# RWKV rounds of a hybrid trunk step emitted phase by phase, and two norm products moved to GpSimd

## The chip, the cores and the metric

The kernel runs on one core of one Trainium2 chip. The metric is the device time of one execution in microseconds (us); the kernel before was run three times. The engines are named as in the profile: PE is TensorE's matmul, PEld its weight load, DVE is VectorE, ACT is ScalarE, POOL is GpSimd, and SP (SyncE) issues most of the transfers.

## The reference

One step of a trunk of two layers. The even layer runs differential attention and a bidirectional RWKV-7 time mixing side by side; the change touches the RWKV part alone. For 1280 positions (1024 latent tokens in four blocks of 256, and 256 context tokens), 8 heads of 64 and two directions it computes:

```python
def wkv_scan(state0, r, w, k, v, kk, a):
    def step(S, inp):
        r_t, w_t, k_t, v_t, kk_t, a_t = inp
        sa = jnp.einsum("bhij,bhj->bhi", S, -kk_t)
        S = (S * w_t[:, :, None, :] + sa[..., None] * (kk_t * a_t)[:, :, None, :]
             + v_t[..., None] * k_t[:, :, None, :])
        return S, jnp.einsum("bhij,bhj->bhi", S, r_t)
...
    for d in range(2):
        w_raw = (P["rwkv_w0"][e, d] + jnp.tanh(wd[:, :, d]) @ P["rwkv_w2"][e, d]).astype(jnp.float32)
        decay = jnp.exp(-jnp.exp(-jax.nn.softplus(-w_raw) - 0.5))
        a = jax.nn.sigmoid(P["rwkv_a0"][e, d] + ad[:, :, d] @ P["rwkv_a2"][e, d])
        kd = k * (1 + (a - 1) * kvec[1])
...
        S, y = wkv_scan(s0[:, d], *inputs)
...
        ys = ys + y
        bonus = bonus + jnp.sum(rh * kdh * r_k, axis=-1, keepdims=True) * vh
    mu = jnp.mean(ys, axis=-1, keepdims=True)
    var = jnp.mean((ys - mu) ** 2, axis=-1, keepdims=True)
    yn = ((ys - mu) * lax.rsqrt(var + LNX_EPS)).reshape(b, L, B_WIDTH)
    y = (yn * lnx[0] + lnx[1] + bonus.reshape(b, L, B_WIDTH)).astype(fb.dtype) * g
```

## The kernel before

The scan is done in chunks of 32 positions. The RWKV stage has **five rounds**, q = 0 to 4. A round takes 256 positions of each direction (round 4 the context), which are 8 chunks of 8 heads in two directions. A round is split in two **halves** of four heads (half number n = 2q and 2q + 1), a half in two **pairs** of units (pair pp_ = 0, 1; a unit is two heads of one direction d).

The parts of a round, each written as a Python generator that yields between its pieces:

- **Preparation** of a half, `half_prep`: two pairs, each with two `unit_values` and two `unit_products`, so four steps a pair. A unit loads r, k and kkh (`piece_prep`; in rounds 0, 1 and 4, which are called fresh here, kkh is worked out: head sums L746/L808, a root with GpSimd's power L137, rsx L817, a flip on TensorE L753, kkh L820). Then come the small products lora_ps (L760, tanh on ScalarE L764), the scan sc (L842) and bk (L868, L874) on VectorE, kr, bkw and others on GpSimd (L839 to L878), the matrices G_ps (L897, masked into G on VectorE L901), the copies il (L904) and bd (L884) on ScalarE, bonus sums bon_ps (L746, L909) and flips of bkw (L753, copied into G on ScalarE L914).
- **Inverse** of the round, `inverses`: one VectorE chain of 31 steps over all units of the round. Each step has a product tm (L947) and an addition into x (L951), both with (31-kk)(kk+1) elements in 128 partitions. It begins with two transposes nn (L937, L938) and ends with xt and xn (L957, L958). It needs il of both halves.
- **Corrections** of a half, `corrections`: for each of four units GpSimd copies tz out of xt or xn (L984), and TensorE does mq_ps (L988), gv_ps (L993), ms_ps (L1000) and tb_ps (L1006), with ScalarE copies between. They load sv (L978).
- **Chains** of a half, `chains`: four steps, each with L1052 on TensorE, L1057 on VectorE, L1061 on TensorE, the new state (L1076) on VectorE, and the outputs y_ps (L1085, L1090) on TensorE. Chain 0 is the first half's, chain 1 the second half's. In round 4 a chain ends with four transposes of the states (sf_ps, L1113) and their stores (L1118).
- **Posts**, `post(q, d)`: the group norm of a finished block of 256 positions, done during the inverse of the next round (posts of round 2 in round 3, of round 3 in round 4; the last one behind round 4). It reads the array y (128 x 1024) and the values vb. Mean and variance are VectorE's (L1157), GpSimd does vb times the bonus (L1150), plus the bias (L1152) and the power ln_r (L137), and VectorE does y times ln_r (L1159), times the weight (L1160), plus vb (L1161) and, behind flips on TensorE, the gate product ob (L1168).
- **ada**: the blocks of adaLN weights. Each block has two 512 KB loads (ada_w, SP's queue, two buffers), matmuls L191, a copy L196 and small matmuls L200. It fills in wherever a `run` names it, so many steps a round.

`run` takes pairs of a generator and a count and interleaves their steps in proportion. What it emits is the program's order of priority. A scheduler then reorders the instructions of each engine by a simulated timeline, so the order on an engine is not the order of the code. All PSUM tiles of preparation, posts, corrections, ada and the states come from `ps_g`, one ring of three buffers that are handed out in the order of emission: a tile cannot be written before the one emitted three places earlier was read.

In a round, `pa_` is the preparation of the next round's first half, `pb_` that of its second half, `co[0]` and `co[1]` are the corrections of the halves, and `ch[0]` and `ch[1]` the chains. Before, pair 1 of `pa_` (four of its nine steps) is emitted beside the inverse, one step beside `co[0]`, and the other four beside chain 0 and `co[1]`. Half of `pb_` goes beside chain 1, the rest behind it.

Of the kernel before, what the change touches and what calls it, by code (L numbers as in the profile page):

```python
# [15 lines left out]
ALU = mybir.AluOpType  # L16
# [83 lines left out]
def hybrid_step(ctx: ExitStack, tc: tile.TileContext, i: dict, o: dict):  # L100
    nc = tc.nc
# [232 lines left out]
    with ExitStack() as st:  # L334
# [45 lines left out]
        with ExitStack() as st2:  # L380
            wp = pool(st2, "wv", side="right")
            for cb in range(4):
                raw = ww.tile([128, KD, 128], F32, tag="w_raw", bufs=3, name="v_raw")
                with tc.issue_after(first_ada):
                    nc.sync.dma_start(
                        out=raw,
# [7 lines left out]
                if cb % 2 == 1:  # L394
                    for ti in range(T // 128):
# [11 lines left out]
                        if ti >= LS // 128:  # L407
                            r0 = ti * 128 - LS
                            nc.gpsimd.dma_start(
                                out=o["cache_v"][0, 0, r0:r0 + 128].rearrange("t h d -> t (h d)")[:, cs], in_=vs  # L410
# [3 lines left out]
        with ExitStack() as st2:  # L414
# [35 lines left out]
            def do_fb(ti):  # L450
# [38 lines left out]
                out=nlam[:, 1:2], in0=ls[:, 0:1], scalar1=ls[:, 1:2], scalar2=LAM_INIT, op0=ALU.subtract, op1=ALU.add  # L489
# [177 lines left out]
    with ExitStack() as st:  # L667
# [26 lines left out]
        for a, x in enumerate((0.5, -0.5)):  # L694
# [6 lines left out]
            out=kv1h[:, 1, :], in0=kv[:, 1, :], scalar1=-0.25, scalar2=0.5, op0=ALU.mult, op1=ALU.add  # L701
# [2 lines left out]
        for p in range(4):  # L704
            nc.vector.tensor_scalar(out=bonk[:, p, :], in0=bones, scalar1=kv[:, 2, p:p + 1], scalar2=2.0, op0=ALU.mult, op1=ALU.mult)
        NP, NTP, NCP = 256, 2, 4
        A1, A2, A3, A4, A5 = 18, 4, 6, 6, 16
        cmask = eg.tile([128, NP], F32, name="cmask")
        nc.gpsimd.memset(cmask, 1.0)
        nc.gpsimd.memset(cmask.rearrange("p (c s) -> p c s", s=C)[:, :, 0:1], 0.0)  # L710
# [414 lines left out]
        def post(q, d):  # L1125
# [8 lines left out]
            vb = lt.tile([128, NTP, 512], F32, tag="vb", bufs=1, name="vb")  # L1134
# [4 lines left out]
            yf = y.rearrange("p a b s -> p a (b s)")  # L1139
# [11 lines left out]
            lv = lambda a: cst["lnx"][:, a, :].unsqueeze(1).to_broadcast([128, NTP, 512])  # L1151
# [5 lines left out]
                nc.vector.reduce_sum(var[:, a:a + 8], sq, axis=AX.X)  # L1157
            rsqrt(rs, var, 1.0 / 64, LNX_EPS, lt, NH2)
            nc.vector.tensor_tensor(out=yv, in0=yv, in1=bc(rs), op=ALU.mult)  # L1159
            nc.vector.tensor_tensor(out=yf, in0=yf, in1=lv(0), op=ALU.mult)  # L1160
            nc.vector.tensor_tensor(out=yf, in0=yf, in1=vb, op=ALU.add)  # L1161
            yield
            for p in range(4):
                gp = ps_g([128, NP], "gg_ps")
# [8 lines left out]
        def run(*gens):  # L1173

            todo = [[g, n, 0] for g, n in gens if n]
            while todo:
                t = min(todo, key=lambda t: (t[2] + 1) / t[1])
                t[2] += 1
                if next(t[0], 0) == 0 or t[2] == t[1]:
                    todo.remove(t)  # L1180

        none = iter(())
        ada = ada_blocks(
            [(0, j) for j in range(8, 24)] + [(1, j) for j in range(24)], ep, PG[0], "ada", 1, 2, 1
        )
# [16 lines left out]
        for q in range(5):  # L1202
            inv = inverses(R[q])
            pa_ = begin(2 * q + 2)
            ps_ = chain(*[post(*a) for a in posts.get(q - 1, ())])
            run((inv, 9), (pa_, 4), (ada, A1), (ps_, 16))
            if q == 4:
                for _ in ada:
                    pass
            co = [corrections(R[q], H[2 * q + e]) for e in range(2)]  # L1210
            ch = [chains(H[2 * q + e]) for e in range(2)]
            run((inv, 9), (co[0], 4), (pa_, 1), (ada, A2))
            y_tiles(q)
            run((ch[0], 5), (co[1], 4), (pa_, 4), (ada, A3))
            if q == 4:
                st_d.close()
                PG[:] = [pool(st, "pz", space=PSUM), 2]
                fw = pool(st_w, "fw1", side="right")
                out_weights(fw, pool(st_o, "ow", side="right"), range(KD))
                fo = pool(st_o, "of", side="right")  # L1220
                po = pool(st_o, "po", space=PSUM, side="right")
            pb_ = begin(2 * q + 3)
            run((ch[1], 5), (pb_, 2), (ada, A4))
            run((pb_, 9), (ada, A5))
        fs = [out_product(fw, fo, po, 128 * j) for j in range(1)]
        run((post(4, 0), 9))

# [276 lines left out]
    with ExitStack() as st:  # L1504
# [17 lines left out]
        ps_ = pool(st_p, "qps", space=PSUM, side="right")  # L1522
# [73 lines left out]
        for cnd, (base, L, ntl, nl) in enumerate(SEQ):  # L1596
            nc.vector.tensor_scalar(
                out=z0[:, :, cnd], in0=z0[:, :, cnd], scalar1=1.0 / math.sqrt(L), scalar2=None, op0=ALU.mult
            )
            nc.vector.tensor_scalar(  # L1600
                out=z0[:, :, 2 + cnd], in0=B[:, cnd, :], scalar1=math.sqrt(L), scalar2=None, op0=ALU.mult
# [334 lines left out]
```

## Time and profile before

| | us |
|---|---|
| median of three runs | 3839.11 |
| lowest, highest | 3833.22, 3840.68 |
| profiled execution, its span | 3833.54, 3831.7 |
| busy in the span: PE, DVE, ACT, POOL | 3464.8, 1956.9, 1344.8, 735.4 |
| first transpose nn of rounds 0 to 4 | 809.45, 997.17, 1143.95, 1288.26, 1462.22 |
| xt of rounds 0 to 4 | 858.62, 1039.19, 1183.37, 1343.88, 1510.21 |
| first product of the attention's and RWKV's output projection | 1598.36 |

The times in the profile count from the start of the span. The granted TensorE clock over the whole span is 0.945 of full speed. The RWKV rounds lie between 809 and 1598 us; the rest of the span is projections, attention, token mixing and the gated MLPs, which the change doesn't touch.

### The profile page before, as it was taken

How to read it: one execution, taken by the hardware profiler on the slowest of the kernel's cores; microseconds unless marked ns; L12 is line 12 of the kernel's file. 1: busy time of each engine (PE TensorE's matmuls, PEld its weight loads, DVE VectorE, ACT ScalarE, POOL GpSimd, SP SyncE). 2: the span in 40 equal slices, each digit the busy share in tenths (PEclk: the TensorE clock that was granted, in tenths of full speed). 3: DMA queues.
4: the chain of work that ended last, by engine and by line, in shares of the span. 5: the costliest groups of instructions: out<-in, count | busy, mean ns of one | idle time of the engine just before them, and what ended most of it. 6: DMA issues, size and time to landing. Idle time of an engine off the chain costs nothing.

```text
span 3831.7 us, 54213 instructions
## 1 busy us (share of the span) xinstructions
PE 3464.8 (90%) x21096; PEld 2892.1 (75%) x21096; DVE 1956.9 (51%) x3752; ACT 1344.8 (35%) x2831; POOL 735.4 (19%) x1225
## 2 busy tenths in 40 slices
PE   7999998789687585899999999998968999999997
PEld 5888887558576484788888888887857888888886
DVE  4277676463655846565344434446554344443446
ACT  4266566544453443463211211113443211121211
POOL 3111111443454543153000000004141000000003
PEclk9999999869898796899999999999998999999999
DMA  6332222464421110345111111104341111111113
GB/s 200 105 88 90 90 68 79 132 201 148 142 65 30 53 33 31 119 136 144 39 34 45 34 39 39 39 31 167 130 115 32 39 39 34 43 35 39 39 31 129
DMA packets 331857, 299.38 MB, mean 78 GB/s; under 512 B 52938, under 2 KB 288298, under 8 KB 331600
## 3 DMA queue, kind: packets, MB, share of 16 engines
q1 hardware_dynamic: 267248, 235.81, 20.0%
q0 software_dynamic: 15952, 40.46, 3.1%
q10 hardware_dynamic: 48400, 19.65, 2.0%
q8 instruction: 166, 2.72, 0.3%
q14 instruction: 91, 0.75, 0.1%
HBM read 239.55 MB, written 58.33 MB: 78 GB/s over the span
## 4 chain that ended last, share of the span: by engine, by line
PE 76%; DVE 7%; DMA 5%; ACT 3%; issue 2%; POOL 2%; ACTq 0%; SPq 0%; DVEq 0%; POOLq 0%
PE a_ps L146 10%; PE a_ps L147 10%; PE a_ps L145 10%; PE b_ps L146 5%; PE b_ps L145 5%; PE b_ps L147 5%; PE f_ps L145 2%; PE f_ps L146 2%; PE f_ps L147 2%; PE pv_ps L557 2%; PE tb_ps L1006 2%; PE sc_ps L521 2%; PE G_ps L897 2%; DMA ada_w<-in_w_ada 1%; DVE x L951 1%
## 5 line engine op out<-in xcount | busy, mean ns | idle before, releaser
L145 PE MATMUL a_ps<-hh,f_hi 128*128 128x512 f32 (+1 forms) x2144 | 761.2, 355 | 19.2 <-ACT f_hi L140 15.6
L146 PE MATMUL a_ps<-hl,f_hi 128*128 128x512 f32 (+1 forms) x2144 | 761.8, 356 | 3.1 <-POOL hl L309 3.1
L147 PE MATMUL a_ps<-hh,f_lo 128*128 128x512 f32 (+1 forms) x2144 | 760.6, 355 | 0.2 <-DVE f_lo L141 0.2
L1351 DVE TENSOR_TENSOR acc<-b_ps,acc 128x512 f32<-128x512 f32 x400 | 270.3, 688 | 405.9 <-PE b_ps L147 405.9
L145 PEld LDWEIGHTS a_ps<-hh,f_hi 128*128 128x128 f32 x2144 | 404.2, 189 | 83.7 <-ACT f_hi L140 16.2
L146 PEld LDWEIGHTS a_ps<-hl,f_hi 128*128 128x128 f32 x2144 | 404.1, 189 | 68.7 <-POOL hl L309 5.1
L147 PEld LDWEIGHTS a_ps<-hh,f_lo 128*128 128x128 f32 x2144 | 404.6, 189 | 63.1 <-DVE f_lo L141 0.9
L146 PE MATMUL b_ps<-d_lo,mh 128*128 128x512 f32 x880 | 348.3, 396 | 0.0
L147 PE MATMUL b_ps<-d_hi,ml 128*128 128x512 f32 x880 | 346.8, 394 | 0.0
L145 PE MATMUL b_ps<-d_hi,mh 128*128 128x512 f32 x880 | 341.5, 396 | 3.6 <-DVE acc L1351 3.1
L1297 POOL MEMSET gp<- 128x1 f32 x44 | 4.3, 98 | 1572.1 <-DVE cv L1316 1572.1
L141 DVE TENSOR_TENSOR f_lo<-f_raw,f_hi 128x512 fp32r<-128x512 f32 x176 | 114.3, 689 | 308.3 <-ACT f_hi L140 306.1
L140 ACT CAST d_hi<-d_raw 128x512 fp32r<-128x512 f32 x88 | 54.5, 621 | 489.0 <-PE b_ps L147 474.9
L145 PE MATMUL f_ps<-hh,w_hi 128*128 128x512 f32 (+1 forms) x552 | 199.3, 361 | 0.5 <-ACT nk L445 0.5
L145 PEld LDWEIGHTS b_ps<-d_hi,mh 128*128 128x128 f32 x880 | 165.2, 188 | 44.9 <-DVE acc L1351 4.5
L146 PE MATMUL f_ps<-hl,w_hi 128*128 128x512 f32 (+1 forms) x552 | 197.9, 359 | 0.0
L147 PE MATMUL f_ps<-hh,w_lo 128*128 128x512 f32 (+1 forms) x552 | 197.9, 358 | 0.0
L147 PEld LDWEIGHTS b_ps<-d_hi,ml 128*128 128x128 f32 x880 | 164.9, 187 | 40.7
L146 PEld LDWEIGHTS b_ps<-d_lo,mh 128*128 128x128 f32 x880 | 165.1, 188 | 37.3
L1308 ACT COPY gp<-a_ps 128x512 f32<-128x512 f32 (+1 forms) x134 | 68.0, 507 | 338.6 <-PE a_ps L147 338.6
L1328 DVE TENSOR_TENSOR md<-a_ps,cv 128x512 f32<-128x512 f32 (+1 forms) x134 | 79.5, 595 | 164.8 <-PE a_ps L147 100.3
L140 ACT CAST f_hi<-f_raw 128x512 fp32r<-128x512 f32 x176 | 101.2, 620 | 156.2 <-PE a_ps L146 147.5
(566 smaller groups left out, 6826.9 us busy)
## 6 DMA issues: line engine op xcount, KB each, us to landing
ada_w<-in_w_ada SPq DMA_DIRECT2D x96, 512.0 KB, 4.8
f_raw<-in_w_ffn_in SPq DMA_DIRECT2D x176, 256.0 KB, 3.2
d_raw<-in_w_ffn_out SPq DMA_DIRECT2D x88, 256.0 KB, 2.8
nx<-x_d SPq DMA_DIRECT2D x24, 512.0 KB, 5.3
w_raw<-in_w_in_even SPq DMA_DIRECT2D x23, 512.0 KB, 4.1
rx<-x_d SPq DMA_DIRECT2D x20, 512.0 KB, 5.4
fb_d<-fsh POOLq DMA_DIRECT2D x15, 512.0 KB, 3.2
qr<-q_d ACTq DMA_DIRECT2D x80, 64.0 KB, 2.3
```

What stands on the lines that cost most here:

```text
L140: nc.scalar.copy(hi, src)
L141: nc.vector.tensor_tensor(out=lo, in0=src, in1=hi, op=ALU.subtract)
L145: nc.tensor.matmul(ps, lhsT=a[0], rhs=b[0], start=first, stop=False)
L146: nc.tensor.matmul(ps, lhsT=a[0], rhs=b[1], start=False, stop=False)
L147: nc.tensor.matmul(ps, lhsT=a[1], rhs=b[0], start=False, stop=last)
L521: nc.tensor.matmul(ps[:, :nn], lhsT=qs[:, m, a, :], rhs=ks[m][:, n0:n0 + nn], start=(a == 0), stop=(a == 1),)
L557: nc.tensor.matmul(pv, lhsT=wt[:, kb, :], rhs=vt[:, kb, :], start=(kb == 0), stop=(kb == nk // 128 - 1))
L897: nc.tensor.matmul(ps[:, c, :], lhsT=bd[:, c, h, :], rhs=kr[:, c].rearrange("p a s -> p (a s)"), start=True, stop=True,)
L1006: nc.tensor.matmul(ps[:, e, h, :], lhsT=tz[:, c + e, h, :], rhs=g[:, c + e, h, 64:192], start=True, stop=True,)
L1308: nc.scalar.copy(gp[:, o0:o0 + n], up(ws, t0, n))
L1328: nc.vector.tensor_tensor(out=md, in0=ps, in1=cv[:, o0:o0 + n], op=ALU.mult)
L1351: nc.vector.tensor_tensor(out=acc[j][:, cs], in0=ps, in1=acc[j][:, cs], op=ALU.add)
```

## The change

Three edits. The round's `run` calls name whole parts one after the other: all nine steps of `pa_` are emitted beside the inverse and the posts; then `co[0]` alone, `ch[0]` alone, `co[1]` with ada, half of `pb_`, `ch[1]` alone, and the rest of `pb_` with ada. The ada steps of a round are dealt out as 25, 10 and 15 instead of 18, 4, 6, 6 and 16 (50 in both). And in `post` two products of 128 x 1024 elements, L1160 and L1161, go from VectorE to GpSimd.

```diff
-        A1, A2, A3, A4, A5 = 18, 4, 6, 6, 16
+        A1, A2, A3 = 25, 10, 15
...
-            nc.vector.tensor_tensor(out=yf, in0=yf, in1=lv(0), op=ALU.mult)
-            nc.vector.tensor_tensor(out=yf, in0=yf, in1=vb, op=ALU.add)
+            nc.gpsimd.tensor_tensor(out=yf, in0=yf, in1=lv(0), op=ALU.mult)
+            nc.gpsimd.tensor_tensor(out=yf, in0=yf, in1=vb, op=ALU.add)
...
-            run((inv, 9), (pa_, 4), (ada, A1), (ps_, 16))
+            run((inv, 9), (pa_, 9), (ada, A1), (ps_, 16))
...
-            run((inv, 9), (co[0], 4), (pa_, 1), (ada, A2))
+            run((inv, 9), (co[0], 4))
             y_tiles(q)
-            run((ch[0], 5), (co[1], 4), (pa_, 4), (ada, A3))
+            run((ch[0], 5))
+            run((co[1], 4), (ada, A2))
...
             pb_ = begin(2 * q + 3)
-            run((ch[1], 5), (pb_, 2), (ada, A4))
-            run((pb_, 9), (ada, A5))
+            run((pb_, 2))
+            run((ch[1], 5))
+            run((pb_, 9), (ada, A3))
```

What the scheduler makes of it is seen in the order of the built programs. **TensorE in round 0**, just ahead of the first correction (L988 on mq_ps), as a piece of the difference, where + marks rows that are new at this place:

```order
+L760 MATMUL lora_ps<-lo_in,w2s 128x256 x2
+L191 MATMUL ada_ps<-ada_w,csil 32x256 x4
+L897 MATMUL G_ps<-kr,bd_7351 128x128 x8
+L746 MATMUL bon_ps<-bonk,ta 128x2 x2
+L200 MATMUL ada_ps_11570<-sel,ada_mp 128x2 x2
+L753 MATMUL fl_ps<-ident,bkw 128x128 x4
+L191 MATMUL ada_ps<-ada_w,csil 32x256 x8
+L897 MATMUL G_ps<-kr,bd_7350 128x128 x8
+L746 MATMUL bon_ps<-bonk,ta 128x2 x2
+L200 MATMUL ada_ps_11664<-sel,ada_mp 128x2 x2
 L753 MATMUL fl_ps<-ident,bkw 128x128 x4
 L988 MATMUL mq_ps<-tz_7352,G 64x32 x8
```

Before, the last flip of pair 1 stood right ahead of L988; now the whole of pair 2 and 32 matmuls of L191 (eight loads of ada_w) stand between. On VectorE the rows up to xt and xn are the same as before in this round, and pair 2's come behind them.

**VectorE in round 2**, in the second half of the inverse, where before only L947 and L951 took turns from this place on:

```order
L868 SCALAR_TENSOR_TENSOR bk<-ta,kkh 128x4x64
L947 TENSOR_TENSOR tm<-nn,x 128x256
L842 SCALAR_TENSOR_TENSOR sc<-cmask,th 128x256
L951 TENSOR_TENSOR x<-x,tm 128x16x16
L868 SCALAR_TENSOR_TENSOR bk<-ta,kkh 128x4x64
L947 TENSOR_TENSOR tm<-nn,x 128x255
L842 SCALAR_TENSOR_TENSOR sc<-cmask,th 128x256
L951 TENSOR_TENSOR x<-x,tm 128x17x15
L854 TENSOR_TENSOR e_11538<-sc 128x4x64
```

Pair 2 stands between the inverse's steps 15 to 28; the same holds in round 1. In both, pair 2 is gone from chain 0, and the second half's corrections are still interleaved with chain 0 on TensorE.

**GpSimd in round 3**, behind the first copies tz out of xt and xn and ahead of the first L997 of the corrections. Before:

```order
L984 COPY tz_7352<-xt 32x8x32 x2
L984 COPY tz_7353<-xn 32x8x32 x2
L941 MEMSET x 128x1024
L942 MEMSET x 128x32
L997 COPY G<-sv_7355 64x8x64
```

Now 22 more instructions stand between the same two (the middle twelve of them):

```order
L839 TENSOR_SCALAR th<-th 128x256
L137 TENSOR_TENSOR ln_r<-ln_r,eps_c 128x16
L872 TENSOR_TENSOR bk<-ta,k 128x4x64
L861 COPY wcol<-e_13063 128x4
L863 TENSOR_TENSOR kr<-kkh,e_13063 128x4x64
L864 TENSOR_TENSOR kr<-r,e_13063 128x4x64
L873 TENSOR_TENSOR ta<-bk,r 128x256
L1160 TENSOR_TENSOR y<-y,lnx 128x1024
L878 TENSOR_TENSOR bkw<-bk,wcol 128x512
L1161 TENSOR_TENSOR y<-y,vb 128x1024
L839 TENSOR_SCALAR th<-th 128x256
L1150 TENSOR_TENSOR vb<-vb,bon 128x1024
```

They are pair 2 of the last half but one to be prepared (half 8) and parts of the posts. On TensorE the products of pair 2 and the flips of the posts stand ahead of round 3's first L988 as well. In round 4, which has nothing to prepare, the posts stand ahead of L988 as before, and the second half's corrections stand behind the whole of chain 0 and its four sf_ps, where before they were interleaved with chain 0.

## The prediction

> **What bounds the kernel now.** I read the page's busy shares first, then the busy time by stage (a view of windows), because the change touches only the five RWKV rounds. Round q = 0 to 4 has an inverse stage (from the transposes L937 to the transpose xt, L957) and a stage of corrections and chains. Here are both stages of rounds 0, 2 and 3 and the second one of round 1, with columns time, length, busy time and count by engine, granted TensorE clock, DMA share, GB/s:
>
> ```profile
> 809.40:861.70 52.30, 41.37 (x270) 27.27 (x271) 39.72 (x99) 20.93 (x54) 15.91 (x22) 0.67 0.59 180
> 861.70:997.10 135.40, 126.82 (x1407) 102.99 (x1407) 56.39 (x172) 63.98 (x131) 56.69 (x87) 0.95 0.57 174
> ...
> 1042.20:1143.90 101.70, 90.94 (x1043) 81.31 (x1042) 45.27 (x117) 51.98 (x101) 50.60 (x81) 0.95 0.20 64
> 1143.90:1186.40 42.50, 13.94 (x82) 12.28 (x81) 38.49 (x82) 13.12 (x25) 15.77 (x20) 0.67 0.06 19
> 1186.40:1288.20 101.80, 91.69 (x1048) 81.92 (x1047) 52.80 (x127) 50.56 (x98) 49.36 (x80) 0.95 0.14 40
> 1288.20:1346.90 58.70, 24.45 (x90) 17.50 (x89) 55.60 (x102) 17.23 (x36) 29.69 (x25) 0.59 0.19 54
> 1346.90:1462.20 115.30, 98.27 (x1046) 88.39 (x1046) 54.04 (x128) 54.38 (x105) 53.75 (x82) 0.90 0.09 28
> ```
>
> An inverse stage is VectorE's: 38.49 of 42.50 us busy in round 2, 55.60 of 58.70 in round 3. A stage of corrections and chains is TensorE's: 126.82 of 135.40, 90.94 of 101.70, 91.69 of 101.80 and 98.27 of 115.30 us. The rule for this change follows. Work that leaves the chains gives back its TensorE time, and work that goes into the inverse costs its VectorE time. Work that stands between the two, with nothing beside it, costs its whole latency.
>
> **Rounds 1 and 2: pair 2 moves into the inverse.** A half's preparation is two pairs of units; before, pair 2 ran beside chain 0. In round 2 the first 14 steps of the inverse run with pair 1 between them and the last 14 alone. The steps' sizes are symmetric (row kk has (31-kk)(kk+1) elements), so these two windows hold equal inverse work:
>
> ```profile
> 1150.20:1170.30 20.10, 8.75 (x48) 8.33 (x48) 18.85 (x42) 8.20 (x15) 10.76 (x16) 0.66 0.14 40
> 1173.05:1183.37 10.32, 0.00 (x0) 0.00 (x0) 9.36 (x29) 0.00 (x0) 0.00 (x0) 0.50 0.00 0
> ```
>
> 20.10 against 10.32 us: a pair in the inverse costs **9.8 us**. The order shows pair 2 from step 15 on, where it pays the same. What the chains gain is TensorE time. The groups of round 0's second stage (three pairs: pair 2 and both pairs of the second half) have the price of a pair:
>
> ```profile
> L191 PE MATMUL ada_ps<-ada_w,csil 128*32 128x256 f32 x256 | 23.4, 412 | 4.3 <-DMA ada_w<-in_w_ada 2.8 <-DVE sc L842 1.2 <-DVE mod L203 0.3
> L897 PE MATMUL G_ps<-kr,bd 128*128 128x128 f32 x88 | 13.0, 299 | 1.7 <-ACT bd L884 1.2 <-issue 0.5
> ...
> L200 PE MATMUL ada_ps<-sel,ada_mp 128*128 128x2 f32 x64 | 9.3, 249 | 0.0
> ...
> L760 PE MATMUL lora_ps<-lo_in,w2s 128*128 128x256 f32 x24 | 6.9, 415 | 0.0
> L746 PE MATMUL kk_ps<-bones,sq 128*128 128x2 f32 x24 | 3.5, 251 | 0.0
> L753 PE MATMUL fl_ps<-ident,bkw 128*128 128x128 f32 x20 | 3.2, 283 | 0.0
> L753 PE MATMUL fl_ps<-ident,rsx 128*128 128x128 f32 x12 | 2.9, 325 | 0.0
> L753 PE MATMUL fl_ps<-ident,v 128*128 128x128 f32 x12 | 2.6, 295 | 0.0
> L746 PE MATMUL bon_ps<-bonk,ta 128*128 128x2 f32 x20 | 2.5, 231 | 0.0
> ```
>
> Products, LoRA, flips of bkw and bonus sums: (13.0 + 6.9 + 3.2 + 2.5) / 3 = **8.5 us** a pair; with the fresh rounds' head sums and flips of v and rsx (2.9 + 2.6 + 3.5 more) **11.5 us**. Rounds 1 and 2 each lose 9.8 and gain 8.5: +1.3, together **+2.6 us** (-8 to +8: the waits that go with the pair's products may go too, or the first correction may wait for its last G).
>
> **Round 0: pair 2 stands between.** Here the order keeps VectorE's row up to xt unchanged and puts pair 2 behind it; on TensorE it stands ahead of the first correction (L988), with 8 ada loads (32 rows of L191 in the order; the profile counts each twice, 8 to a load). The mechanism is the PSUM ring of ps_g: three buffers handed out in the order of emission, so the corrections' mq_ps waits for everything emitted before. Its cost has two bounds. The loads come at the pace of the inverse stage:
>
> ```profile
> 809.40:861.70 52.30, 12.74 (x112) 2.92 (x112) 0.67 0.59 180
> ```
>
> 112 matmuls are 14 loads in 52.3 us, 3.74 us each, so 8 loads hold the first correction back by 29.9 us. The latency of a fresh pair alone is seen ahead of round 0, from its first square to the second unit's copy into G:
>
> ```profile
> 714.98 0.51 ACT L806 ACTIVATE sq<-k,kv 128x256 f32<-128x256 f32 x1 [3.46 <-DMA kv<-in_rwkv_kvec]
> ...
> 739.28 0.58 ACT L914 COPY G<-fl_ps 128x512 f32<-128x512 f32 x1
> ```
>
> 739.28 + 0.58 - 714.98 = 24.9 us, for loads had in time. I take 28, between them. The chains give back 11.5 for the pair, and for the 8 loads 23.4 x 64/256 + 9.3 x 1/4 = 8.2 us (a load has 8 of the 256 matmuls of L191, and 4 blocks of two loads have 16 of the 64 of L200). Sum: 28 - 19.7 = **+8.3 us** (0 if the pair takes 25 and some of the stage's 8.6 us of TensorE waits go too; +18 if the loads set 30 and the two more that now stand in the round's tail come at 3.74 each).
>
> **Round 3: pair 2 and half of a post stand between.** Before, post(2,0) and most of post(2,1) were in the inverse, and the first correction began soon after xt:
>
> ```profile
> 1343.88 1.25 DVE L957 STREAM_TRANSPOSE xt<-x 128x1024 f32<-128x1024 f32 x1
> ...
> 1349.35 1.09 PE L988 MATMUL mq_ps<-tz,G 128*64 128x32 f32 x16
> ```
>
> Now pair 2 (fresh) and post(2,1) stand behind xt. VectorE's groups of that stage, and GpSimd's:
>
> ```profile
> L1160 DVE TENSOR_TENSOR y<-y,lnx 128x1024 f32<-128x1024 f32 x2 | 2.9, 1456 | 0.0
> L1168 DVE TENSOR_TENSOR ob<-fl_ps,ob 128x256 f32<-128x256 f32 x7 | 2.9, 411 | 0.4 <-PE fl_ps L753 0.3
> L1157 DVE TENSOR_REDUCE ln_v<-sq_ps 128x8 f32<-128x512 f32 x4 | 2.7, 684 | 0.0
> L1159 DVE TENSOR_TENSOR y<-y,ln_r 128x1024 f32<-128x1024 f32 x2 | 2.4, 1221 | 0.1
> L1161 DVE TENSOR_TENSOR y<-y,vb 128x1024 f32<-128x1024 f32 x2 | 2.4, 1214 | 0.0
> L137 POOL TENSOR_TENSOR ln_r<-ln_r,eps_c 128x16 f32<-128x16 f32 x2 | 6.0, 2978 | 8.6 <-DVE ln_r L135 8.5
> L1152 POOL TENSOR_TENSOR vb<-vb,lnx 128x1024 f32<-128x1024 f32 x2 | 4.7, 2366 | 0.2
> L1150 POOL TENSOR_TENSOR vb<-vb,bon 128x1024 f32<-128x1024 f32 x2 | 3.9, 1947 | 5.7 <-DMA vb<-vtok_d 5.7
> ```
>
> What leaves the inverse on VectorE: two L1157 (1.4), L1159 (1.2), L1160 and L1161 (half of 2.9 + 2.4, 2.7) and three of the seven L1168 (1.2): 6.5 us. GpSimd's products cost VectorE time as well. In the timeline the step of 128x240 beside L1150 and L1152 takes five times what it takes alone:
>
> ```profile
> 1306.36 1.99 POOL L1150 TENSOR_TENSOR vb<-vb,bon 128x1024 f32<-128x1024 f32 x1 [0.40 <-DMA vb<-vtok_d]
> 1306.63 1.99 DVE L947 TENSOR_TENSOR tm<-nn,x 128x240 f32<-128x240 f32 x1
> 1308.43 2.39 POOL L1152 TENSOR_TENSOR vb<-vb,lnx 128x1024 f32<-128x1024 f32 x1
> 1308.93 2.16 DVE L951 TENSOR_TENSOR x<-x,tm 128x240 f32<-128x240 f32 x1
> ...
> 1325.37 0.41 DVE L951 TENSOR_TENSOR x<-x,tm 128x240 f32<-128x240 f32 x1
> ```
>
> (1.99 - 0.41) + (2.16 - 0.41) = 3.3 us a post. So post(2,1) takes 6.5 + 3.3 = 9.8 us with it. For post(2,0), which stays, the products L1160 and L1161 save VectorE 2.7 and by these rows cost it about 3.3 in stopped steps: +0.6, not a gain. The inverse ends at 1343.88 - 1288.2 - 9.2 = 46.5 us into the round instead of 55.7.
>
> The Trainium skill bears on this in "SBUF — State Buffer", section "SBUF: two separate sides": a VectorE operation with two SBUF inputs and a GpSimd operation that reads SBUF lock each other out for a whole instruction. By that rule a product would stop a step for up to its own 2.2 us, so a post would lose 4.4 - 2.7 = +1.7 instead of +0.6; over the three posts that is 3 us more. The rows above agree in kind (1.58 and 1.75 us lost), and I keep theirs.
>
> From xt to the first correction the order puts on GpSimd: pair 2, one ln_r, one L1150, one L1152 and two moved products. The stage had 29.69 us on GpSimd for pair 1 and two posts; less one ln_r (2.98), one L1150 (1.95) and one L1152 (2.37), plus two products at their mean of 2.16 (same 128x1024 shape), that is 26.7 us in one queue, and some 2 for what leads in and out: 29 at least. At most it is the pair's 24.9 and the post's share of GpSimd, 26.7 - (29.69 - 2 x 7.30) = 11.6 us, one after the other, and about 4 of its flips: 41. I take 33, nearer to the queue's own sum: the first correction at 79.5 instead of 61.15, +18.4; less the fresh pair's 11.5 from the chains, **+7 us** (0 to +18).
>
> **Round 4** has no preparation left. Its windows, with the inverse, corrections with chain 0, and the rest up to the out product:
>
> ```profile
> 1462.20:1510.20 48.00, 14.10 (x54) 9.37 (x53) 42.34 (x87) 7.53 (x16) 14.52 (x6) 0.57 0.15 50
> 1510.20:1563.10 52.90, 49.42 (x686) 47.53 (x687) 15.87 (x46) 20.66 (x46) 15.64 (x29) 0.94 0.07 18
> 1563.10:1598.40 35.30, 18.73 (x193) 15.16 (x190) 24.78 (x57) 15.82 (x33) 3.11 (x4) 0.77 0.65 206
> ```
>
> Two posts' products move: 2 x 0.6 = +1.2 on the inverse. The order also separates the second half's corrections from chain 0 (the state transposes at its end now come first in the ring). That stage was 93% TensorE (49.42 of 52.90), so chain 0 alone leaves gaps. In the last window chain 1 runs alone and TensorE is idle for 16.57 us, the waits for weights among them; half of that, 8.3, is my upper bound, and below nothing stands -4, if the two products' stops miss VectorE's steps. What follows is set by the weight loads (206 GB/s in the last window), which the order puts behind the half's last loads of sv, about where they are now, so I take +2.8 of the 8.3: in all **+4 us** (-4 to +12).
>
> **Sum.** 2.6 + 8.3 + 7 + 4 = +22 us. The profiled execution took 3833.54 us (span 3831.7); the median of the three runs is 3839.11, 5.6 more. Its own time would become 3855.5; on the median, which I use, 3861.
>
> **The rivals.**
> (1) *Pair 2 is mostly hidden.* TensorE and ScalarE are idle behind xt, and its loads are there; if the pair needs 17 us, not 25 to 28, and the ada loads come faster with the chains' transfers gone, round 0 gives -3 and round 3 +3: 3861 - 15 = 3846. For it: 8.75 us of TensorE in the 20.1 us window of pair 1. Against it: eight loads at 3.74 us and GpSimd's 26.7.
> (2) *Faster: the waits go with the pair.* The chain stages of rounds 0 to 3 hold TensorE idle for 8.6, 10.8, 10.1 and 17.0 us, 46.5 together. If the pair's chain through three engines is what makes them, and three quarters go, the time is 3861 - 35 = 3826. It decides from 30 / 4 = 7.4 us a stage. Against it: the second half's pairs still run beside chain 1 and cause the same waits.
> (3) *The order hardly differs* because the scheduler reorders anyway: 3839. The order of the built kernels speaks against it.
> (4) *Both held-back rounds reach their upper bounds:* +18 and +14 in place of +8.3 and +7: 3878 to 3880.
>
> **How the numbers follow.** Chances: forecast 0.57, (1) 0.20, (2) 0.07, (3) 0.04, (4) 0.12. The range is 3838 to 3884: up to rival (4) with round 4's upper end, down to the sum with rounds 1 and 2 at -8 and rival (1). About 0.2% (7.7 us) is what a measurement of this kernel can tell from no change, so "same" is 3831.4 to 3846.8: rival (3), half of (1) and a tail of the forecast, 0.15; faster 0.07; slower 0.78.
>
> **What would show it.** In the new profile: round 0's first L988 some 28 us behind xt, and pair 2's products ahead of it; the inverses of rounds 1 and 2 at 52 us instead of 42 to 45 and their chain stages 8 to 9 us shorter; in round 3 xt about 9 us earlier and the first L988 some 33 us behind it with GpSimd busy throughout; VectorE's steps of 2 us beside L1160 and L1161. Wrong would be: a first correction within 15 us of xt in rounds 0 and 3, or chain stages shorter by much more than a pair's TensorE time.

## The result, and the profile after

The changed kernel took 3866.15 us (median of four runs, 3865.10 to 3876.00) against 3836.98 us of the kernel before (3833.22 to 3840.68), run alongside: 29 us slower by the medians. The ratio on record is **1.0082**, 95% interval 1.0062 to 1.0102; it is worked out from all runs and not from the medians, whose quotient is 1.0076. The profiled execution has a span of 3864.4 us instead of 3831.7.

These are the windows of the changed kernel's profile: for rounds 0 and 3 the inverse, the wait from xt to the first correction (L988), and the stage of corrections and chains; for rounds 1 and 2 the inverse with its short wait, and that stage (columns as in the prediction):

```profile
803.87:851.12 47.25, 37.08 (x249) 23.50 (x249) 36.39 (x97) 19.94 (x51) 14.78 (x20) 0.71 0.64 196
851.12:881.02 29.90, 23.98 (x162) 16.35 (x161) 14.92 (x36) 15.82 (x32) 15.98 (x24) 0.71 0.63 195
881.02:995.96 114.94, 105.37 (x1246) 87.31 (x1245) 46.62 (x138) 48.01 (x101) 40.19 (x64) 0.96 0.49 149
995.96:1051.31 55.35, 32.54 (x209) 26.28 (x209) 50.25 (x103) 26.51 (x51) 23.74 (x36) 0.75 0.34 107
1051.31:1145.45 94.14, 82.75 (x995) 76.82 (x996) 39.47 (x104) 41.96 (x82) 41.95 (x66) 0.91 0.18 57
1145.45:1199.11 53.66, 25.16 (x129) 22.01 (x127) 47.99 (x95) 23.77 (x44) 26.91 (x35) 0.70 0.12 35
1199.11:1293.39 94.28, 82.55 (x989) 76.82 (x990) 46.62 (x114) 40.55 (x79) 40.57 (x65) 0.90 0.11 32
1293.39:1343.09 49.70, 21.95 (x96) 16.84 (x96) 46.11 (x90) 14.57 (x29) 25.26 (x22) 0.60 0.16 46
1343.09:1385.02 41.93, 19.72 (x86) 15.47 (x86) 20.15 (x29) 15.79 (x31) 27.46 (x28) 0.62 0.21 60
1385.02:1485.97 100.95, 85.49 (x972) 79.01 (x972) 45.54 (x105) 40.88 (x82) 38.59 (x61) 0.90 0.06 16
1485.97:1538.07 52.10, 14.79 (x49) 8.95 (x47) 48.91 (x84) 7.52 (x16) 24.68 (x11) 0.55 0.13 42
1538.07:1624.15 86.08, 69.06 (x873) 63.11 (x873) 34.83 (x96) 34.95 (x75) 16.90 (x31) 0.94 0.26 81
```

Two stages are new: 29.90 us in round 0 and 41.93 us in round 3, between xt and the first correction. In neither is an engine busy throughout: in round 0 TensorE has 23.98 us of work, in round 3 it has 19.72, VectorE 20.15, GpSimd 27.46. The stages of corrections and chains behind them are shorter than before (114.94 for 136.2, 100.95 for 112.9), and so are those of rounds 1 and 2, whose inverses are longer. In these two stages the granted clock is lower than before (0.91 and 0.90; 0.94 and 0.95 before), but L988's matmuls are no slower: the 128 in each take 223 ns in the median, in both kernels.

Set side by side for the kernel before, the changed one and the first experiments (the others' stages stand with their runs), with the boundaries nn (L937), xt (L957), the first L988 and the next nn (in round 4 the first product of the output projection), in us:

| kernel | R0 inverse + wait + chains | R1 | R2 | R3 | R4 | rounds |
|---|---|---|---|---|---|---|
| before | 49.2 + 2.3 + 136.2 | 42.0 + 2.0 + 102.8 | 39.4 + 2.0 + 102.9 | 55.6 + 5.5 + 112.9 | 48.0 + 2.0 + 86.2 | 788.9 |
| before, once more | 46.1 + 2.4 + 135.7 | 42.0 + 2.0 + 102.8 | 39.5 + 2.0 + 102.9 | 55.7 + 5.5 + 112.9 | 47.5 + 2.0 + 86.2 | 785.0 |
| changed | 47.2 + 29.9 + 114.9 | 53.4 + 2.0 + 94.1 | 51.7 + 2.0 + 94.3 | 49.7 + 41.9 + 101.0 | 50.1 + 2.0 + 86.1 | 820.3 |
| products back | 48.4 + 29.4 + 120.1 | 55.6 + 2.0 + 93.3 | 51.3 + 2.0 + 93.9 | 52.3 + 27.0 + 101.2 | 47.6 + 2.0 + 90.2 | 816.1 |
| products only | 49.3 + 2.3 + 139.2 | 40.2 + 2.0 + 105.2 | 39.5 + 2.0 + 103.9 | 55.4 + 13.5 + 110.0 | 50.2 + 2.0 + 89.2 | 803.9 |
| round 3 as before | 46.5 + 29.3 + 117.6 | 55.4 + 2.0 + 94.2 | 51.7 + 2.0 + 94.3 | 55.4 + 13.5 + 111.3 | 50.4 + 2.0 + 90.4 | 815.9 |
| round 0 as before | 48.1 + 2.4 + 137.1 | 51.3 + 2.0 + 94.3 | 51.0 + 2.0 + 95.7 | 50.1 + 41.2 + 97.1 | 50.1 + 2.0 + 89.5 | 813.8 |

From before to changed the rounds have +4.4, +2.7, +3.6, **+18.6** and +2.1 us. The two executions also differ by -5.6 us ahead of round 0, where the order on VectorE, ScalarE and GpSimd is the same; "before, once more" starts its rounds 2.4 us earlier than "before", so a few us there are spread. Behind round 4 they differ by +6.9 us. There the order isn't the same: the last post stands there, with its two products on GpSimd too. From the first output product to the end, the six profiled kernels with these products on GpSimd take 2234.2 to 2240.2 us, and the six with them, but not L1150 and L1152, on VectorE 2230.9 to 2234.1, 4.0 less in the mean. So a part of the 6.9 is probably the change's; it isn't shown, since the two kernels with all four products on VectorE take 2235.7 and 2236.8. Rounds 1 to 3 of the kernel before repeat within 0.2 us, rounds 0 and 4, which wait for weights, within some 4.

### The profile page after: what moved, and what is told of

Same layout as the page of the kernel before. It is cut to its first block, busy times and chain, and to the rows that moved or that the text cites. A ratio compares the mean times of both kernels' runs of the same rounds, so it can differ in the third digit from the quotient of the medians.

```text
span 3864.4 us, 54242 instructions
## 1 busy us (share of the span) xinstructions
PE 3474.1 (90%) x21096; PEld 2904.0 (75%) x21096; DVE 1977.9 (51%) x3742; ACT 1346.3 (35%) x2831; POOL 761.5 (20%) x1235
## 4 chain that ended last, share of the span: by engine, by line
PE 53%; DVE 3%; DMA 2%; issue 1%; ACT 1%; POOL 1%; ACTq 0%; DVEq 0%; SPq 0%; POOLq 0%
PE a_ps L146 10%; PE a_ps L147 10%; PE a_ps L145 10%; PE b_ps L146 5%; PE b_ps L145 5%; PE b_ps L147 5%; PE o_ps L145 1%; PE o_ps L146 1%; PE o_ps L147 1%; DMA x_d<-nx 1%; DVE acc L1380 0%; PE xt_ps L1549 0%; PE ab_ps L1561 0%; PE tb_ps L1006 0%; DVE x L951 0%
## 5 line engine op out<-in xcount | busy, mean ns | idle before, releaser
L897 PE MATMUL G_ps<-kr,bd 128*128 128x128 f32 x640 | 109.9, 341 | 66.4 <-ACT bd L884 46.9
L1330 DVE TENSOR_TENSOR md<-a_ps,cv 128x512 f32<-128x512 f32 (+1 forms) x134 | 79.6, 596 | 165.5 <-PE a_ps L147 101.0
```

Source lines behind the costliest of these rows:

```text
L897: nc.tensor.matmul(ps[:, c, :], lhsT=bd[:, c, h, :], rhs=kr[:, c].rearrange("p a s -> p (a s)"), start=True, stop=True,)
L1330: nc.vector.tensor_tensor(out=md, in0=ps, in1=cv[:, o0:o0 + n], op=ALU.mult)
```

## The experiments

Ratios are to runs of the kernel before on the same chip. Each theory is told in the text on record.

### The two halves of the change, one at a time

`e1_products_back` is the changed kernel with the products on VectorE again:

```diff
-            nc.gpsimd.tensor_tensor(out=yf, in0=yf, in1=lv(0), op=ALU.mult)
-            nc.gpsimd.tensor_tensor(out=yf, in0=yf, in1=vb, op=ALU.add)
+            nc.vector.tensor_tensor(out=yf, in0=yf, in1=lv(0), op=ALU.mult)
+            nc.vector.tensor_tensor(out=yf, in0=yf, in1=vb, op=ALU.add)
```

> The changed kernel with L1160 and L1161 back on VectorE; the phase by phase emission stays. Theory A (round 3's wait of 41.9 us from xt to the first correction is the post's chain on GpSimd, ln_r, L1160, L1161, with pair 2's second unit behind the flips of y on TensorE): two products 2.3 to 1.2 us each and no queueing behind pair 2's GpSimd work, so the wait falls to 36 to 38 us; rounds 3 and 4's inverses 1 to 2 us shorter. In all 6 to 9 us faster than the changed kernel: 3857 to 3860. Rival B (the wait is pair 2's own latency in a ring of three buffers): the wait stays at 41 to 42, in all 2 to 3 us faster, 3863.

3854.77 us, ratio 1.0049 (1.0032 to 1.0066). That is theory A's side: 13 us faster than the changed kernel by the ratios, 8 by the medians against those of before, where A had 6 to 9. Round 3's wait fell to 27.0 us, much further than either theory had it, and the round from 192.6 to 180.4, though its inverse took 2.6 us more and not 1 to 2 less. Round 4's inverse fell by 2.5.

`e2_products_only` is the opposite: the kernel before with the diff of these two lines the other way round.

> The kernel before with only the two products moved to GpSimd. Theory A (a GpSimd product stops the VectorE step beside it for its whole length): inverses of rounds 3 and 4 1 to 4 us longer each, in all 2 to 8 us slower than before. Rival B (VectorE is relieved of 2.4 us a post): the inverses of rounds 3 and 4 2 to 5 us shorter each, in all 4 to 10 us faster than before.

3841.93 us, ratio 1.0018 (1.0008 to 1.0029): the total is theory A's. Round 4's inverse took 50.2 us instead of 48.0 and 47.5. In round 3, though, the inverse was no longer at all (55.4); the wait behind it grew, from 5.5 to 13.5. So in round 3, where A had 1 to 4 us on the inverse, the price isn't the stopped steps but the place where the post ends.

The four kernels make a table of two by two. Round 3: 174.0 before, 179.0 with the products only, 180.4 with the emission only, 192.6 with both. Alone they cost 5 and 6.4 us; together 18.6, 7 more than the sum. `e6_round0_as_before`, with both in its round 3, has 188.4 there, so 3 more than the sum. The ratios, 1.0018, 1.0049 and 1.0082, are in the same order, but their intervals are too wide to show by themselves that the two parts do more than add up.

### Where round 3 waits

The timeline of round 3 in the changed kernel, from xt to the first correction (in brackets idle time of the engine just before, and what ended it):

```profile
1343.09 1.25 DVE L957 STREAM_TRANSPOSE xt<-x 128x1024 f32<-128x1024 f32 x1
...
1354.65 2.92 POOL L137 TENSOR_TENSOR ln_r<-ln_r,eps_c 128x16 f32<-128x16 f32 x1 [1.49 <-DVE ln_r L135]
...
1357.61 1.74 DVE L1159 TENSOR_TENSOR y<-y,ln_r 128x1024 f32<-128x1024 f32 x1 [3.04 <-POOL ln_r L137]
...
1361.32 2.33 POOL L1160 TENSOR_TENSOR y<-y,lnx 128x1024 f32<-128x1024 f32 x1
...
1364.34 1.04 POOL L878 TENSOR_TENSOR bkw<-bk,wcol 128x512 f32<-128x512 f32 x1 [0.69 <-DVE bk L874]
1365.34 2.34 POOL L1161 TENSOR_TENSOR y<-y,vb 128x1024 f32<-128x1024 f32 x1
1367.73 0.69 PE L753 MATMUL fl_ps<-ident,y 128*128 128x128 f32 x2 [13.89 <-POOL y L1161]
1368.21 1.91 PE L760 MATMUL lora_ps<-lo_in,w2s 128*128 128x256 f32 x4
...
1379.74 3.75 PE L897 MATMUL G_ps<-kr,bd 128*128 128x128 f32 x16 [3.40 <-POOL kr L864]
...
1385.02 1.92 PE L988 MATMUL mq_ps<-tz,G 128*64 128x32 f32 x16
```

TensorE stands still for 13.89 us until GpSimd has done L1161, because the flip of y is next in its order. Pair 2's second unit, whose LoRA product L760 needs nothing of the post, is queued behind that flip. It begins at 1368.21 and its last products end at 1383.5, 15.3 us later; the first correction stands behind those. On GpSimd the post's two products stand among pair 2's, L878 between them, and take 2.33 and 2.34 us. With the products on VectorE (`e1_products_back`) the same chain is:

```profile
1354.70 2.92 POOL L137 TENSOR_TENSOR ln_r<-ln_r,eps_c 128x16 f32<-128x16 f32 x1 [1.67 <-DVE ln_r L135]
1354.77 1.25 DVE L957 STREAM_TRANSPOSE xt<-x 128x1024 f32<-128x1024 f32 x1
...
1359.43 1.73 DVE L1160 TENSOR_TENSOR y<-y,lnx 128x1024 f32<-128x1024 f32 x1
...
1361.20 1.58 DVE L1161 TENSOR_TENSOR y<-y,vb 128x1024 f32<-128x1024 f32 x1
...
1362.93 0.66 PE L753 MATMUL fl_ps<-ident,y 128*128 128x128 f32 x2 [9.23 <-DVE y L1161]
1363.38 1.91 PE L760 MATMUL lora_ps<-lo_in,w2s 128*128 128x256 f32 x4
```

From the root's start to the flip it takes 8.2 us (1362.93 - 1354.70) instead of 13.1 (1367.73 - 1354.65), and the root starts at xt, not 11.6 us behind it. So of the 14.9 us by which the wait is shorter 4.9 are the two products with what stands between them, and the larger part is that the root comes earlier, measured from xt; why the built order has it so late in the changed kernel isn't shown. `e2_products_only` has the same wait of TensorE without any pair 2 held back; there 32 matmuls of L897 fall between xt and the first correction, where before 16 did:

```profile
1341.02 2.34 POOL L1161 TENSOR_TENSOR y<-y,vb 128x1024 f32<-128x1024 f32 x1
1343.41 0.69 PE L753 MATMUL fl_ps<-ident,y 128*128 128x128 f32 x2 [14.40 <-POOL y L1161]
```

`e3_round3_as_before` emits round 3 alone as before (the other calls alike, with the old counts):

```diff
+            old = q == 3
-            run((inv, 9), (pa_, 9), (ada, A1), (ps_, 16))
+            run((inv, 9), (pa_, 4 if old else 9), (ada, 18 if old else A1), (ps_, 16))
...
+            if old:
+                run((ch[0], 5), (co[1], 4), (pa_, 4), (ada, 6))
```

> The changed kernel with round 3 alone emitted as before (pair 2 and the second half's corrections beside chain 0), products on GpSimd. Theory A (most of the loss is the work held between xt and the first correction of round 3): round 3 falls from 192.6 to 174 to 177 us and the whole to 3849 to 3852. Rival B (held work only moves the loss, the chains then cost as much more): 3858 or more.

3860.81 us, ratio 1.0075 (1.0054 to 1.0097). Round 3 fell by 12.3 us, to 180.3, not to A's 174 to 177: what is left is the products' price (`e2_products_only`, with the same emission there, has 179.0). The total is on B's side: A's 3849 to 3852 would be a ratio of 1.0031 to 1.0039. The profile's rounds are only 4.4 us shorter, since rounds 0, 1 and 4 were longer by 1.3, 2.1 and 4.5. Round 4 took 139.8 to 142.9 us in place of 138.2 in the four kernels measured together here (this one, `e1_products_back`, `e2_products_only` and `e4_post2_light`); `e8_all_beside_chains`, from the same chip and with round 4 emitted as before, has 135.8, so the chip alone isn't the reason. So the loss in round 3 is where A has it, and how much of it the whole gets back by this edit stays open.

`e4_post2_light` takes the post's long chain out of round 3, so that it no longer computes the same values there:

```diff
+            if q != 2:
                 nc.gpsimd.tensor_tensor(out=vv, in0=vv, in1=bc(bo), op=ALU.mult)
...
+            if q != 2:
                 rsqrt(rs, var, 1.0 / 64, LNX_EPS, lt, NH2)
```

> The changed kernel with the posts of round 2 (done in round 3) without L1150, L1152, the root ln_r, L1159, L1160 and L1161: the values go unnormed to the flips and the gate product, so what they compute is changed. Theory A (the post's chain holds pair 2's second unit): the wait from xt to the first correction in round 3 falls from 41.9 to 24 to 27 us, the latency of a pair alone, and the inverse loses 10 us: in all 24 to 28 us faster than the changed kernel. Rival B (pair 2's own latency in the ring): the wait stays above 35 us, in all about 15 us faster.

3839.64 us, ratio 1.0016 (1.0006 to 1.0026), so about 25 us faster than the changed kernel, as A says, though not in the way I had told: without that work the scheduler put most of pair 2 into the inverse (54.1 us), and the wait was 4.8 us, not 24 to 27. Round 3 took 159.0. It doesn't measure a pair alone, and part of the gain is the work left out. It does show that pair 2 doesn't hold the corrections without this part of the post; whether the chain's length or its engine time kept pair 2 out of the inverse isn't separated.

### Round 0, and the ring

`e6_round0_as_before` is the same edit as in `e3_round3_as_before` with `old = q == 0`.

> The changed kernel with round 0 alone emitted as before. Theory A (pair 2 and eight ada loads between xt and the first correction cost 27 us there and give 21 back in the chains): round 0 falls from 192.1 to 187 to 189 us, the whole by 3 to 6 us. Rival B (round 0 costs nothing net, the 4.4 us are the spread of one execution): no change of round 0 beyond 1 us.

3861.42 us, ratio 1.0072 (1.0053 to 1.0092). Round 0 took 187.6 us instead of 192.1: theory A. The whole is 4 us faster by the ratios, less than their intervals can tell, and one execution says little about round 0. The four profiled kernels with the new emission in round 0 have 192.1 to 197.8 us, mean 195.3; the five with the old one (both of before, `e2_products_only`, this one, and `v3_before_posts_on_vector` below, 188.1) have 184.1 to 190.8, mean 187.7. The means differ by 7.6.

TensorE's own waits for the loads in the changed kernel's stretch are short, as its timeline shows:

```profile
861.81 1.08 PE L191 MATMUL ada_ps<-ada_w,csil 128*32 128x256 f32 x8 [1.29 <-DMA ada_w<-in_w_ada]
864.20 1.08 PE L191 MATMUL ada_ps<-ada_w,csil 128*32 128x256 f32 x8 [0.37 <-DMA ada_w<-in_w_ada]
867.14 1.08 PE L191 MATMUL ada_ps<-ada_w,csil 128*32 128x256 f32 x8 [0.35 <-DMA ada_w<-in_w_ada]
```

Idle times of 1.29, 0.37 and 0.35 us, 2.0 in all: the loads were nearly in time, though 8 of them stand in this stretch. TensorE is busy for 23.98 of the 29.90 us, with pair 2 and the ada blocks, so the loads' pace set little of the stretch. How much shorter it would be without the ada blocks wasn't tried.

`e7_ring_apart` gives the corrections a PSUM ring of their own, one buffer, and leaves two to the rest:

```diff
-        PG = [pool(st_d, "pg", space=PSUM, side="right"), 3]
+        PG = [pool(st_d, "pg", space=PSUM, side="right"), 2]
...
         def ps_g(shape, name):
+            if name in ("mq_ps", "gv_ps", "ms_ps", "tb_ps"):
+                return PG[0].tile(shape, F32, tag="k", bufs=1, name=name)
```

> The changed kernel with the corrections' PSUM tiles (mq, gv, ms, tb) in a ring of their own with one buffer, and two buffers left for the rest. Theory A (the ring of three in emission order is what keeps the first correction behind pair 2): the first correction comes within 10 us of xt in rounds 0 and 3; round 3 falls from 192.6 to below 185. What the smaller rings cost elsewhere isn't known: each correction's four tiles then go one by one, which may cost 1 to 2 us a unit, 40 units. Rival B (the order comes from priorities, not from the ring): the first correction stays 30 and 42 us behind xt.

3850.91 us, ratio 1.0050 (1.0031 to 1.0068). In its windows the first correction follows xt within 2 us in round 0 and about 5 in round 3; these are round 0's inverse, wait and chains, and round 3's inverse and wait:

```profile
817.70:865.80 48.10, 37.72 (x224) 22.34 (x224) 34.55 (x91) 16.56 (x45) 14.89 (x21) 0.65 0.63 197
865.80:867.75 1.95, 0.84 (x5) 0.47 (x5) 1.95 (x3) 1.80 (x3) 0.71 (x2) 0.63 0.22 67
867.75:985.97 118.22, 114.98 (x1288) 90.87 (x1289) 50.52 (x147) 61.87 (x129) 54.82 (x87) 0.98 0.65 198
...
1285.37:1355.55 70.18, 41.01 (x265) 30.28 (x264) 63.52 (x139) 22.29 (x44) 29.77 (x30) 0.70 0.13 38
1355.55:1360.61 5.06, 0.00 (x0) 0.00 (x0) 5.06 (x4) 1.04 (x1) 5.01 (x3) 0.50 0.00 0
```

1.95 us instead of 29.90 and 5.06 instead of 41.93, with the same emission: it is the ring that held the corrections, as theory A says. Round 0 took 168.3 us, round 3 174.7. In round 3 part of what the wait lost went into the inverse, 70.2 us instead of 49.7, so the first correction comes 16.4 us earlier in the round, not 36.9. Given back: round 4 took 166.1 us instead of 138.2 (that there the corrections have no other work beside them to fill the time between their tiles is the likely reason; with a second buffer `v1_ring_apart_tuned` has 140.6), and the preparation ahead of round 0 took longer (round 0 starts at 817.7 instead of 803.9). The profiled execution is the slowest of its five, 11.6 us above the median.

`e7b_before_ring_apart` is the same edit on the kernel before.

> The kernel before with the corrections' PSUM tiles in a ring of their own with one buffer, and two buffers for the rest: the price of the smaller rings by themselves, to be set against the run of the changed kernel with the same rings. If the ring's size matters, each chain stage is 5 to 15 us longer than before; if not, the time is that of before within 0.2%.

3853.43 us, ratio 1.0044 (1.0029 to 1.0059). Neither case: rounds 0 to 3 took 165.8, 152.0, 147.0 and 168.9 us, 19 less than before in all, and round 4 took 167.4, 31 more. With rings apart the two kernels hardly differ (1.0050 and 1.0044): rounds 0 to 3 of the changed one take 8.7 us more in all, where with the shared ring it is 29.3. So it is the shared ring that made the emission matter.

### More of what the change did in rounds 1 and 2, and its opposite

There pair 2 went into the inverse: the inverses took 11.4 and 12.3 us more and the stages behind gave 8.7 and 8.6 back. `e8_all_beside_chains` goes the other way and takes pair 1 out of the inverse as well:

```diff
-            run((inv, 9), (pa_, 4), (ada, A1), (ps_, 16))
+            run((inv, 9), (ada, A1), (ps_, 16))
...
-            run((inv, 9), (co[0], 4), (pa_, 1), (ada, A2))
+            run((inv, 9), (co[0], 4), (pa_, 2), (ada, A2))
...
-            run((ch[0], 5), (co[1], 4), (pa_, 4), (ada, A3))
+            run((ch[0], 5), (co[1], 4), (pa_, 7), (ada, A3))
```

> The kernel before with all of the next first half's preparation beside corrections and chains, none beside the inverse. By the exchange seen in rounds 1 and 2 (a pair in the inverse costs 11.4 to 12.3 us there and gives 9.6 us back in the chains): 2 to 3.6 us faster in each of rounds 1 and 2, in all 5 to 12 us faster than before. Rival (TensorE's stage is full, and with TensorE idle in the inverse its clock falls, so that the stage behind costs more): same or slower than before by up to 10 us.

3860.27 us, ratio 1.0062 (1.0046 to 1.0078): the rival's side, and by more than it had. Round 1's inverse and its stage of corrections and chains, and below them that stage before:

```profile
1016.20:1045.22 29.02, 2.64 (x18) 2.35 (x16) 25.62 (x67) 1.82 (x3) 0.00 (x0) 0.56 0.00 1
1047.20:1162.56 115.36, 101.16 (x1107) 91.26 (x1108) 52.93 (x130) 63.24 (x122) 62.51 (x98) 0.94 0.21 63
...
1041.16:1143.95 102.79, 92.03 (x1051) 82.40 (x1052) 46.31 (x117) 52.00 (x102) 51.25 (x82) 0.94 0.20 63
```

The inverse alone takes 29.02 us, 13.0 less than with pair 1, and the chains 115.36, 12.6 more; round 2 has -10.4 and +13.5, round 3 -11.1 with its wait and +16.1, round 0 -7.2 and +28.0. The rival's reason, a lower clock, doesn't show in round 1: 0.94 is granted in both stages. TensorE has 9.1 us more work there and stands idle 3.4 us longer. In the inverse a pair thus costs 10 to 13 us, the first (13.0 and 10.4) like the second (11.4 and 12.3). In the chains the first costs 8.7 and 8.6, the second 12.6 and 13.5. Over rounds 1 to 3 one pair in each place, as before, is the cheapest of the three, 465 us against 473 here; in round 1 alone the two are level (146.8 and 146.4). A part of round 0's loss is work from elsewhere: 39 ada loads' matmuls stand behind its xt instead of 32, and none in round 1 instead of 6. The rest wasn't looked into.

### A version that is faster than both

The stages with rings apart point to one. `v1_ring_apart_tuned` keeps the emission of before and the corrections' own buffer, but lets the preparation ahead of round 0 use all three, and round 4's corrections take turns with the buffer that ada has left:

```diff
+            if name in ("mq_ps", "gv_ps", "ms_ps", "tb_ps"):
+                turn[0] += 1
+                tag = "ada" if turn[1] == 4 and turn[0] % 2 else "k"
+                return PG[0].tile(shape, F32, tag=tag, bufs=1, name=name)
+            if turn[1] < 0:
+                turn[0] += 1
+                if turn[0] % 3 == 0:
+                    return PG[0].tile(shape, F32, tag="k", bufs=1, name=name)
```

> The kernel before with the corrections' PSUM tiles in a buffer of their own in rounds 0 to 3 and two buffers for the rest, but without what the smaller rings cost at both ends: ahead of round 0 the preparation uses all three, and in round 4 the corrections take turns between their own buffer and the one that the ada blocks have left. By the stage times of the run with rings apart (rounds 0 to 3 together 633.7 us instead of 652.8), 10 to 20 us faster than before. Rival (round 0's 22 us are ada work that only moves to the stages beside it): within 0.2% of before.

3827.66 us, ratio 0.9995 (0.9982 to 1.0007): the rival. The rounds take 777.9 us instead of 788.9 and 785.0, but start at 815.7 instead of 809.5 and 807.1.

`v2_v1_posts_on_vector` and `v3_before_posts_on_vector` move L1150 and L1152 to VectorE, in `v1_ring_apart_tuned` and in the kernel before:

```diff
-            nc.gpsimd.tensor_tensor(out=vv, in0=vv, in1=bc(bo), op=ALU.mult)
+            nc.vector.tensor_tensor(out=vv, in0=vv, in1=bc(bo), op=ALU.mult)
...
-            nc.gpsimd.tensor_tensor(out=vb, in0=vb, in1=lv(1), op=ALU.add)
+            nc.vector.tensor_tensor(out=vb, in0=vb, in1=lv(1), op=ALU.add)
```

> The run above with the post's two other GpSimd products, L1150 and L1152, on VectorE, so that none is left there. If a GpSimd product stops the VectorE step beside it for its whole length (3.3 to 3.5 us a post against 2.4 on VectorE itself), 2 to 6 us faster than the run above; if VectorE's own time counts, 5 to 10 us slower.

3822.60 us, ratio **0.9976** (0.9964 to 0.9988), 9 us faster than before and 5 faster than `v1_ring_apart_tuned`: the side of the stopped steps, and the one kernel here that beats both. That the stopped steps are the reason isn't shown; the next run makes the same move without this gain.

> The kernel before with L1150 and L1152 on VectorE, the opposite of the change's move. Theory A (stopped steps and GpSimd's queue): inverses of rounds 3 and 4 shorter by 1 to 3 us each, in all 0 to 6 us faster than before. Rival B (VectorE's load sets the inverse): 2.4 us a post longer, 8 to 10 us slower.

3832.82 us, ratio 1.0006 (0.9993 to 1.0018): no difference that this shows, so no sign of B's 8 to 10 us and no gain for A either. Round 4's inverse fell to 46.1 us, round 3's rose to 56.5 with its wait down from 5.5 to 2.0.

> The kernel before once more, for the spread of its stages between two profiled executions: by the earlier runs, rounds 1 to 3 within 2 us, rounds 0 and 4, which wait for loads of weights, within 5.

It is the second row of the table; only round 0 moved by more than half a us, by 3.6.

## Why the prediction was right, and where its sizes were off

The direction and the mechanism held: pair 2 stands between xt and the first correction in rounds 0 and 3, through the ring, and costs more there than the chains give back. That 3866 lies so close to the 3861 of the forecast is partly luck. The forecast was +22 us on 3839.11, and the runs alongside show +29 on 3836.98; and of the terms below, taken from the two profiles (+31.4 in all), round 3 came out 11.6 us and rounds 1 and 2 3.7 us above the forecast, rounds 0 and 4 3.9 and 1.9 below it. By its own steps:

- **Rounds 1 and 2, +2.6 forecast, +6.3 measured.** The chains gave back 8.7 and 8.6 us for 8.5 forecast. The inverse's price was mis-sized: 9.8 from the windows of pair 1, but 11.4 and 12.3 for pair 2.
- **Round 0, +8.3 forecast, +4.4 measured** in this execution, and +7.6 between the means of all profiled kernels. The wait was 29.9 us where I took 28; the chains gave 21.3 for 19.7, with nine loads gone from them, not eight. I had left out the 2.3 us that the first correction waited before, and the inverse was 1.9 shorter in this execution. That the wait equals the 29.9 us of eight loads at 3.74 each is a coincidence: TensorE waited 2.0 us for loads in it.
- **Round 3, +7 forecast, +18.6 measured: the term that was mis-sized.** The chains gave back 11.9 for 11.5, and xt came 5.9 us earlier where I had 9.2. The wait was 41.9 us where I took 33. GpSimd's sum was right (27.46 us busy, 26.7 worked out), but GpSimd was not the bound, and the sign that it would be busy throughout didn't come. I had leaned to its queue, though the order also showed the flips of y on TensorE ahead of pair 2's last products; the upper end, the pair and the post one after the other, came out at 41. With the products on VectorE the wait is 27.0, so the moved products are worth 14.9 us of it (12.2 of the round, whose inverse is 2.6 longer then), through where the post ends ahead of TensorE's flip and not through VectorE's stopped steps.
- **Round 4, +4 forecast, +2.1 measured**, all of it in the inverse. Chain 0 standing alone cost nothing that shows in this execution (86.1 us against 86.2).
- **A product on GpSimd costs VectorE more than it saves.** I had +0.6 us a post; round 4's inverse, with two posts, took 50.1 to 50.4 us in the five profiled kernels with the shared ring and the products on GpSimd, and 47.5 to 48.0 in the four with that ring that have only L1150 and L1152 there (both executions of before, `e1_products_back`, `e8_all_beside_chains`), so 1.1 to 1.4 a post. The steps beside the moved products in round 4 of the changed kernel, and behind them the same two steps in round 2 before, where GpSimd had nothing to do:

```profile
1497.73 2.34 POOL L1160 TENSOR_TENSOR y<-y,lnx 128x1024 f32<-128x1024 f32 x1 [1.39 <-issue]
1497.88 2.38 DVE L951 TENSOR_TENSOR x<-x,tm 128x175 f32<-128x175 f32 x1
1500.15 2.34 POOL L1161 TENSOR_TENSOR y<-y,vb 128x1024 f32<-128x1024 f32 x1
1500.30 2.40 DVE L947 TENSOR_TENSOR tm<-nn,x 128x192 f32<-128x192 f32 x1
...
1178.27 0.36 DVE L947 TENSOR_TENSOR tm<-nn,x 128x192 f32<-128x192 f32 x1
...
1179.43 0.34 DVE L951 TENSOR_TENSOR x<-x,tm 128x175 f32<-128x175 f32 x1
```

Each step lasts about as long as the product beside it, 2.38 and 2.40 us instead of 0.34 and 0.36. That is nearer to the Trainium skill ("SBUF — State Buffer", "SBUF: two separate sides": the second of the two waits for the whole of the first instruction) than to my 1.6 to 1.75 us. By its rule a post would have lost 1.7 us; the measured 1.1 to 1.4 lie between.

A fifth post stands behind round 4 and its products move too; my sum has no term for it, and the stretch behind round 4, with +6.9 us, may hold some of its price.

Two things in the text ahead of the prediction need mending. The ada blocks have a PSUM buffer of their own in that pool and are not in the ring of three, so the eight loads ahead of round 0's first correction are there by the scheduler's order and not by the ring. And the ring as the reason for the corrections' place was argued from the order then; `e7_ring_apart` has shown it since.

Rival (2) of the prediction, that the waits go with the pair, is answered by rounds 1 and 2: their stages lost 8.7 and 8.6 us, a pair's TensorE time and no more. Rival (4), that both held-back rounds reach their upper bounds, came true in round 3 alone: +18.6 us there, where it had +14, but +4.4 in round 0, where it had +18.

## What to carry to other kernels

Where tiles of several parts come from one ring in the order of emission, emitting a part earlier also makes every later part wait for it, whatever else the later part needs; look at what then stands between a chain's end and its successor, and price it at its latency, not its busy time. Two parts that stand one behind the other in an engine's order (here the post's flips and the pair's products on TensorE) can add up even where no engine is full: take the sum of the chains as a bound too, and not the largest engine's sum alone. Moving two elementwise products off a busy VectorE chain onto GpSimd cost more than it saved here, because the two-input steps of VectorE beside them took as long as they did.

## What was not expected of the hardware

What a VectorE step takes beside a GpSimd product followed the product and not the step: steps of 128x175 and 128x192, 0.34 and 0.36 us alone, both lasted 2.4 us beside products of 2.34. Preparation shows it too: bk (L874, 128x512) took 2.81 us beside L1160 in round 3, where the next one took 1.04.
